# Nine split pages for eight, one split in advance, three raw pairs for four, and two query blocks moved behind the query/key blocks

## The chip, the cores and the metric

One core of a Trainium2 chip. The time is the device time of one execution in microseconds (us), smaller is better. TensorE (PE in the profile) multiplies, VectorE (DVE), ScalarE (ACT) and GpSimd (POOL) do the rest, SyncE (SP) issues most of the transfers. All data is float32; the large products run as float32r, in which a value is split into a rounded high part and a low remainder.

## The reference

One layer of a hybrid encoder block on x of 1024 tokens by 1024 channels. Cut to what matters:

```python
h = rms_norm(x, norm_w)
z = einsum('bsd,dc->bsc', h, w_in)          # q, k, v of 3 groups, gates, and the recurrence's inputs
for g, (window, dilation) in enumerate(((128, 1), (512, 4), (2048, 16))):
    q = rms_norm(z_q[g], q_norm_w[g]); k = rms_norm(z_k[g], k_norm_w[g])
    outs, maxes, dens = dilated_window_attention(q, k, v, bias, window, dilation)
o_a = merge(outs, maxes, dens);  y_a = (o_a * silu(g_a)) @ w_proj_a
o_b = rms_norm(scan(q_b, i_b, zf_fwd) + flip(scan(flip(q_b), flip(i_b), flip(zf_bwd)))) * silu(g_b)
y_b = o_b @ w_proj_b
out = x + (sigmoid(zgate_a) * y_a + sigmoid(zgate_b) * y_b) @ w_out
```

There are 24 attention heads of 64 channels (8 in each group) and 8 recurrence heads of 128.

## The kernel before, in words

**Products.** Every large product is made of three float32r matmuls: high by high, high by low, low by high. A weight page of 128 x 512 is loaded raw and split into `whi` and `wlo`. `Builder.split` does it: ScalarE copies the raw page rounded into `whi`; then VectorE or GpSimd subtracts (`b.low` is "dve" or "pool"), or, with `b.low = "dma"`, ScalarE writes minus the high part into `wlo` and GpSimd issues a DMA that adds the page from memory to it. The pages go through two rings of `RING` = 8 buffers, `hir` and `lor`, strictly in order: page k may be split when `k < freed + RING`, where `free_to` counts the pages that TensorE has done with. A ring of `RAWS` = 4 raw pages feeds them; each split asks for the next raw page.

**Order of the work.** The program is laid out by a planner (`Plan`, `Builder`), which books a modelled duration for each instruction and from that decides the order in which each engine gets its instructions. Work waits as a task (an engine, tiles that must be done, a priority, a condition on room) and goes out in `tick`; small products wait in `small` and go out in `burst`. Where a ring has no room, `until` lets modelled time pass until it has. On the chip each engine runs its instructions in the order so laid down and waits on semaphores for its data.

**The stages.** (1) The first value group: `u_products(0, d)` and `u_products(1, d)`, d from 0 to 7, multiply pages 0 to 7 with the unnormalised input of two halves of the tokens; the row scale comes later. After each step d of the second loop page d is freed and, for d under 7, `split_next_page` splits the next one, with `b.low = "dma"`. After the loop `b.auto()` hands the splitting to the planner. (2) The second and third value group (pages 8 to 15 and 16 to 23), in units of eight steps; beside the second, `sums_h` and its followers make the sums of the input's quadrants on VectorE, with `b.low = "dve"`. (3) The blocks, below. (4) The inputs of the recurrence, with the attention of the three groups put in between; the merge of the groups; the recurrence by heads; the two output projections.

**The blocks.** 27 blocks of 1024 tokens by 512 columns (or the like) are computed in seven products instead of eight, in the manner of Strassen. A block's steps are T1, T2, 21, T3, then step 11 of the next block, then 22 and T4; each is 12 matmuls with one split page. `start_quads` loads the raw quarters of a block into pairs from the ring `qraw` (`QRAW` = 4 buffers of 128 x 1024; one pair holds quarters 11 and 12, another 21 and 22) and makes the differences in place on VectorE, each followed by its split; the low parts of T2 and T4 are made on VectorE and the other five on GpSimd. Both pairs of a block are released with its last split, T4. `run_quads` runs the products. Step 11 is evacuated by ScalarE into a buffer p, T1 into c, T2 into u; VectorE adds 21, T3 and 22 to them, and T4 is evacuated by itself. T3 adds into the bank that T2 has been copied from. For query/key blocks p, c and u come from the ring `spare` (`SPARE` = 7 buffers, handed out in turn), for the others from `stage`, and their T4 from `spare`.

There are five kinds of blocks: `qk` (12 of them: queries and keys of a group), `sg` (sigmoid gates), `qb` (the recurrence's queries), `gb` and `ga` (gates that pass through Silu in `put_raw`). The list `blocks` gives their order. By number, from 0:

```
before: qk sg qk qk sg qk qb qk sg qk qb qk sg qk qb qk sg qk qk sg qk gb gb gb gb ga ga
```

**The norm of queries and keys.** Each `qk` block is followed, for each half of the tokens, by a chain: `squares` (ScalarE), `sq_sum`, `sq_high`, `sq_low`, `head_sums` (two matmuls into `nss`), `guess` (ScalarE: Ln, Exp, Square), `newton`, `norm_root` and two times `scaled` on VectorE, then stores to `qkD`. The chain uses a ring `ny` of four buffers: two in `squares`, three in `guess`. `scaled` releases the block's buffers in `spare`; the T4 part is copied into a raw page (`raw<-qA` in the profile). Ln and Exp are called with the table of `natural_log_exp_and_others` loaded at the start of the stage (`blocks_start`); Silu brings in another table.

Of the kernel before, what the change touches and what calls it, by code (L numbers as in the profile page):

```python
# [21 lines left out]
NEG = -1e30  # L22
TABW = 384
WARM = 10
RING = 8
RAWS = 4
LEAD = 4
TAIL, LATE = 4, 4
EARLY = 8
QB = 6  # L30
QRAW, SPARE = 4, 7
RES = (1, 4, 16)
LOWS = ("T2", "T4")
SQ, EA = 2, 6
# [198 lines left out]
class Builder:  # L233
# [94 lines left out]
    def setup_weights(self, items, pool, ring, raws):  # L328
        self.RING = ring
        self.wpages, self.windex, self.quads, self.steps = [], [], [], []  # L330
        n = 0
        for k, it in enumerate(items):
            if not isinstance(it, tuple):
                self.wpages.append(it)
                self.windex.append(n)
                n += 1
                continue
            m = len(self.quads)
            self.quads.append(it)
            more = k + 1 < len(items) and isinstance(items[k + 1], tuple)  # L340
            if k == 0 or not isinstance(items[k - 1], tuple):
                self.steps.append((n, m, "11"))
                n += 1
            for op in ("T1", "T2", "21", "T3", "+", "22", "T4"):
                if op != "+":
                    self.steps.append((n, m, op))
                    n += 1
                elif more:
                    self.steps.append((n, m + 1, "11"))
                    n += 1  # L350
        self.ops = n
        self.w = {}
        self.rawr = self.ring(pool, "raw", raws, [128, 512])
        self.hir = self.ring(pool, "whi", ring, [128, 512], F32R)
        self.lor = self.ring(pool, "wlo", ring, [128, 512], F32R)
        self.raws = []
        self.raw_next = 0
        self.split_next = 0
        self.freed = 0
        self.offered = None  # L360
# [12 lines left out]
    def offer(self, t, k):  # L373
        self.task("act", [t], self.split_next_page, 2, lambda: self.split_next == k and k < self.freed + self.RING)

# [37 lines left out]
    def start_quads(self, ring):  # L413
# [44 lines left out]
        def ready(k):  # L458
            eng, n, m, src, dst = work[k]
            if at[0] != k or (n is not None and (self.split_next != n or n >= self.freed + self.RING)):  # L460
                return False
# [190 lines left out]
def hybrid_block(ctx, tc, a, out):  # L652
    b = Builder(ctx, tc, a)
# [20 lines left out]
    def bank(name):  # L674
        t = b.bank.get(name=name)
        b.bank.done(t)
        return t
# [18 lines left out]
    qk = [("qk", g, hv, e) for g in range(3) for hv in range(2) for e in range(2)]  # L696
    sg = [("sg", 0, j) for j in range(0, 8, 2)] + [("sg", 1, j) for j in range(0, TAIL, 2)]
    blocks = []
    for k in range(6):
        blocks += qk[2 * k:2 * k + 1] + sg[k:k + 1] + qk[2 * k + 1:2 * k + 2] + ([("qb", 2 * k - 2)] if 0 < k <= QB // 2 else [])  # L700
    blocks += [("gb", k) for k in range(4)] + [("ga", 0), ("ga", 2)]

    def block_pages(kind, *at):
# [25 lines left out]
    items += [wpa[i] for i in range(8)]  # L729
    b.setup_weights(items, wpool, RING, RAWS)  # L730

# [83 lines left out]
    def inv_rms(k, ps):  # L815
        for j in range(4):
            t_.matmul(ps[:, j:j + 1], acc[k][:, 128 * j:128 * j + 128], ones[:, 0:1], start=True, stop=True)
        return rsqrt(b, tiny, ps[:, 0:4], 4, 1.0 / D, "x")

    def spread(r):  # L820

        dg = pre.tile([128, 512], F32, tag="sq", name=b.name("dg"), bufs=SQ).rearrange("p (a t) -> p a t", a=4)
        v_.tensor_tensor(dg, ident[:, None, :].to_broadcast([128, 4, 128]),
                                r[:, :, None].to_broadcast([128, 4, 128]), op=OP.mult)
        return dg

    def spread_out(dg):
        ps = bank("rB")
        t_.matmul(ps, ones, dg, start=True, stop=True)
        return ps  # L830
# [164 lines left out]
    def keep_u(j):  # L995
        a_.activation(uv[j], ups[0][j], AF.Copy)
# [18 lines left out]
    def root(k):  # L1015
        rs[k] = inv_rms(k, bank("ss"))
        rs["d", k] = spread(rs[k])

    def root_out(k):
        rs["B", k] = spread_out(rs["d", k])  # L1020
# [16 lines left out]
    for j in range(4):  # L1037
        keep_u(j)
    b.low = "dma"
    at = {0: {11: lambda: root(1)}, 3: {5: lambda: root_out(1), 11: lambda: root(0)}, 7: {5: lambda: root_out(0)}}  # L1040
    for d in range(8):
        u_products(1, d, at.get(d, {}))
# [1172 lines left out]
    def seven_weights(base, pages, order, along=None, by_dma=()):  # L2215
# [13 lines left out]
        def split(op, i):  # L2229
# [3 lines left out]
            def f():  # L2233
# [4 lines left out]
            work.append((op, "act", lambda: (op, i) in raw and b.when_all([raw[op, i]])  # L2238
                         and b.split_next == k and k < b.freed + b.RING, f))

# [321 lines left out]
def _build(arrays):  # L2562
    import concourse.bacc as _bacc
    nc = _bacc.Bacc("TRN2", target_bir_lowering=False, num_devices=1)
    args = {n: nc.dram_tensor(f"in_{n}_dram", v.shape, mybir.dt.from_np(v.dtype), kind="ExternalInput").ap()
            for n, v in arrays.items()}
    out = nc.dram_tensor("out_0_dram", (S, D), F32, kind="ExternalOutput").ap()
    with tile.TileContext(nc) as tc:
        hybrid_block(tc, args, out)
    return nc  # L2570
# [9 lines left out]
```

## Time and profile before

| | |
|---|---|
| median of 3 runs | 1433.92 us (1433.57 to 1437.22) |
| the profiled execution | 1435.38 us; its span, from the first to the last instruction, 1433.6 us |
| mean granted TensorE clock | 0.995 |
| TensorE busy | 1408.3 us, 98% of the span |
| VectorE, ScalarE, GpSimd busy | 918.0, 848.3, 349.5 us |
| bytes moved | 230.31 MB, mean 161 GB/s |

Lines of the profile begin with an engine; `out<-in` are the program's tile names without their numbers, then shapes and a count. A timeline line gives the start in us from the span's start, then the duration, the instruction, and in brackets the idle time before it and what ended it. A line of the list of waits gives the total, the number and the longest. A line of the table by windows gives the window, its length, busy time of PE, weight loads, DVE, ACT and POOL, the granted clock, the DMA share and GB/s. All instructions have the line of one helper, so groups are told by tiles. The blocks run from about 148 to 676 us.

### The profile page before, as it was taken

To read this page: it belongs to the slowest core of one execution; us is meant where nothing else is said; L and a number is where in the kernel's file an instruction comes from. 1 tells how busy PE (TensorE), PEld (TensorE's weight loads), DVE (VectorE), ACT (ScalarE), POOL (GpSimd) and SP (SyncE) were. 2 spreads that over 40 slices of the span, in tenths; PEclk is the share of its full clock that TensorE was granted. 3 is DMA by queue.
4 is the path that set the end of the run, shared out by engine and by line. 5 is a ranking of instruction groups with operands and counts; after the bars stand their busy time and mean duration, and the time that the engine had idled before them with its cause. 6 is when DMAs were issued, how large, how long until landed. Compare 5 with 4: busy or idle time off the path is not lost. (4 is left out here: it accounts for less than half of the span.)

```text
span 1433.6 us, 24071 instructions
## 1 busy us (share of the span) xinstructions
PE 1408.3 (98%) x8506; PEld 1170.7 (82%) x8506; DVE 918.0 (64%) x1890; ACT 848.3 (59%) x1837; POOL 349.5 (24%) x378
## 2 busy tenths in 40 slices
PE   9999999999999999999999999899999999999998
PEld 8778888888888888788778888688888888788887
DVE  6574556666666666542356647978878686358973
ACT  7642656655555565843586642667777684558461
POOL 0100434454433333243141110122123121001011
PEclk9999999999999999999999999999999999999999
DMA  6737566677744434533887239745445443768565
GB/s 225 176 105 212 163 204 160 150 182 174 169 131 118 103 89 98 158 112 117 286 282 254 94 85 273 209 109 126 103 118 126 123 131 87 236 231 220 176 170 143
DMA packets 200804, 230.31 MB, mean 161 GB/s; under 512 B 60531, under 2 KB 125323, under 8 KB 200172
## 3 DMA queue, kind: packets, MB, share of 16 engines
q1 hardware_dynamic: 182876, 193.19, 44.4%
q0 software_dynamic: 16944, 35.40, 13.2%
q8 instruction: 67, 1.10, 0.3%
q14 instruction: 53, 0.43, 0.1%
q10 hardware_dynamic: 864, 0.19, 0.1%
HBM read 168.77 MB, written 81.43 MB: 175 GB/s over the span
## 5 line engine op out<-in xcount | busy, mean ns | idle before, releaser
L60 POOL TENSOR_TENSOR wlo<-qraw,whi 128x512 fp32r<-128x512 f32 x135 | 181.2, 1344 | 390.5 <-ACT whi L60 383.8
L60 ACT ACTIVATE whi<-qraw 128x512 fp32r<-128x512 f32 x189 | 117.7, 626 | 101.6 <-POOL wlo L60 36.8
L60 PE MATMUL gp<-hh,whi 128*128 128x512 f32 x264 | 109.0, 413 | 0.0
L60 DVE TENSOR_TENSOR qraw<-qraw,qraw 128x512 f32<-128x512 f32 x81 | 70.0, 865 | 57.6 <-POOL wlo L60 57.6
L60 PE MATMUL gp<-hh,wlo 128*128 128x512 f32 x264 | 103.6, 392 | 0.0
L60 PE MATMUL gp<-hl,whi 128*128 128x512 f32 x264 | 103.0, 390 | 0.0
L60 ACT ACTIVATE whi<-raw 128x512 fp32r<-128x512 f32 x92 | 57.5, 626 | 75.8 <-DMA raw<-in_w_in_dram 38.3
L60 ACT ACTIVATE as<-as,neg 128x192 f32<-128x192 f32 (+1 forms) x192 | 77.8, 409 | 23.9 <-DVE neg L60 23.9
L60 PE MATMUL qA<-hh,whi 128*128 128x512 f32 x216 | 84.0, 389 | 0.0
L60 PE MATMUL qA<-hl,whi 128*128 128x512 f32 x216 | 84.0, 389 | 0.0
L60 PE MATMUL qA<-hh,wlo 128*128 128x512 f32 x216 | 84.0, 389 | 0.0
L60 PE MATMUL gp<-wlo,hh 128*128 128x512 f32 x192 | 76.0, 396 | 4.0 <-DMA wlo<-in_w_in_dram 3.0
L60 PE MATMUL gp<-whi,hh 128*128 128x512 f32 x192 | 79.6, 415 | 0.0
L60 PE MATMUL gp<-whi,hl 128*128 128x512 f32 x192 | 75.8, 395 | 0.0
L60 POOL COPY mm<-Bc 128x8 f32<-128x8 f32 x64 | 32.5, 543 | 171.6 <-DVE Bc L60 171.6
L60 POOL DMA_DIRECT2D wlo<-in_w_in_dram x36 | 31.1, 864 | 142.1 <-ACT wlo L60 92.3
L60 DVE CUSTOM_DVE_ANT_0 as<-sc,abias 128x192 f32<-128x192 f32 (+1 forms) x192 | 48.4, 308 | 21.3 <-PE sc L60 12.4
L60 PEld LDWEIGHTS gp<-hh,wlo 128*128 128x128 f32 x264 | 49.5, 188 | 10.9
L60 PEld LDWEIGHTS gp<-hh,whi 128*128 128x128 f32 x264 | 49.7, 188 | 8.9
L60 PEld LDWEIGHTS gp<-hl,whi 128*128 128x128 f32 x264 | 49.8, 189 | 8.3
L60 DVE TENSOR_TENSOR wlo<-qraw,whi 128x512 fp32r<-128x512 f32 x54 | 38.4, 711 | 28.2 <-ACT whi L60 28.1
L60 DVE TENSOR_TENSOR ny<-ny,spare 128x512 f32<-128x512 f32 x36 | 55.7, 1549 | 0.0
(316 smaller groups left out, 4123.5 us busy)
## 6 DMA issues: line engine op xcount, KB each, us to landing
raw<-in_w_in_dram SPq DMA_DIRECT2D x84, 256.0 KB, 3.1
qraw<-in_w_in_dram SPq DMA_DIRECT2D x60, 256.0 KB, 4.3
qraw<-in_w_in_dram SPq DMA_DIRECT2D x24, 512.0 KB, 4.4
qkD<-ny SPq DMA_DIRECT2D x192, 64.0 KB, 2.1
wlo<-in_w_in_dram POOLq DMA_DIRECT2D x36, 256.0 KB, 4.4
sg<-sgD SPq DMA_DIRECT2D x32, 256.0 KB, 3.7
eraw<-wsD SPq DMA_DIRECT2D x32, 256.0 KB, 3.1
sgD<-stage SPq DMA_DIRECT2D x26, 256.0 KB, 2.2
```

Source lines behind the costliest of these rows:

```text
L60: got = f(*args, **kw)
```

## The change

`RING` goes from 8 to 9 in all stages: one more buffer in `whi` and one in `wlo`, 2 KB a partition each. `QRAW` goes from 4 to 3: one buffer of 4 KB a partition less in the stage of the blocks. Before the loop over `u_products(1, d)` one page is split in advance, with the low part by DMA. And of the three `qb` blocks that stood between `qk` blocks one stays there (block 9, where the first was block 6), and two go behind the last `qk` block:

```
after:  qk sg qk qk sg qk qk sg qk qb qk sg qk qk sg qk qk sg qk qb qb gb gb gb gb ga ga
```

```diff
-RING = 8
+RING = 9
-QRAW, SPARE = 4, 7
+QRAW, SPARE = 3, 7
...
     for k in range(6):
-        blocks += qk[2 * k:2 * k + 1] + sg[k:k + 1] + qk[2 * k + 1:2 * k + 2] + ([("qb", 2 * k - 2)] if 0 < k <= QB // 2 else [])
+        blocks += qk[2 * k:2 * k + 1] + sg[k:k + 1] + qk[2 * k + 1:2 * k + 2] + ([("qb", 0)] if k == 2 else [])
+    blocks += [("qb", h) for h in range(2, QB, 2)]
     blocks += [("gb", k) for k in range(4)] + [("ga", 0), ("ga", 2)]
...
     for j in range(4):
         keep_u(j)
     b.low = "dma"
+    b.split_next_page()
     at = {0: {11: lambda: root(1)}, ...}
     for d in range(8):
         u_products(1, d, at.get(d, {}))
```

## The prediction

> **What bounds the kernel now.** I read the page first, then the list of what TensorE waits for, then the timelines around its longest waits.
>
> ```profile
> span 1433.6 us, 24071 instructions
> ...
> PE 1408.3 (98%) x8506; PEld 1170.7 (82%) x8506; DVE 918.0 (64%) x1890; ACT 848.3 (59%) x1837; POOL 349.5 (24%) x378
> ```
>
> TensorE is busy 98% of the span. The change adds and removes no matrix product, so it can win only what TensorE loses: 1433.6 - 1408.3 = 25.3 us of idle time and what a lowered clock costs. All the rest is room to lose.
>
> ```profile
> PE kT L60 <- DVE sk L60: 3.9, 1, 3.9
> PE gp L60 <- DMA wlo<-in_w_in_dram: 3.0, 1, 3.0
> PE qA L60 <- ACT stage L60: 2.7, 1, 2.7
> PE sc L60 <- issue: 2.4, 1, 2.4
> PE al L60 <- DVE og L60: 1.8, 1, 1.8
> ```
>
> The columns are total, times, longest: each wait happens once. The second ends on a split page (`wlo`) and the third on ScalarE in the query/key stage: these the change can reach, and a shorter one on `wlo` below. The waits on `sk`, on the scores' first issue and on `og` end on other work of VectorE or on loads of the attention stage; one more split page does not feed them.
>
> **The ninth page and the page split in advance.** The 3.0 us wait, with its neighbours on TensorE, then the window that holds it, then ScalarE and GpSimd ahead of it:
>
> ```profile
> 58.34 0.39 PE L60 MATMUL gp<-whi,hh 128*128 128x512 f32 x1
> 61.68 0.80 PE L60 MATMUL gp<-wlo,hh 128*128 128x512 f32 x1 [2.95 <-DMA wlo<-in_w_in_dram]
> ...
> 65.06 0.40 PE L60 MATMUL gp<-whi,uhi 128*128 128x512 f32 x1
> ...
> 68.93 0.39 PE L60 MATMUL gp<-whi,ulo 128*128 128x512 f32 x1
> ```
>
> ```profile
> 60.00:80.00 20.00, 18.32 (x76) 14.29 (x77) 13.63 (x32) 10.62 (x27) 0.00 (x0) 0.91 0.55 136
> ```
>
> ```profile
> 50.16 0.63 ACT L60 ACTIVATE whi<-raw 128x512 fp32r<-128x512 f32 x1 [0.81 <-PE u L60]
> ...
> 54.96 0.62 ACT L60 ACTIVATE whi<-raw 128x512 fp32r<-128x512 f32 x1
> ```
>
> ```profile
> 51.75 0.86 POOL L60 DMA_DIRECT2D wlo<-in_w_in_dram  x1 [1.86 <-PE u L60]
> 56.54 0.86 POOL L60 DMA_DIRECT2D wlo<-in_w_in_dram  x1 [3.93 <-ACT wlo L60]
> ```
>
> From 65.06 to 68.93 there are 17 steps, 0.228 us each. The ninth matmul after the one at 58.34 would start at 60.39 at that pace and starts at 65.06: the stall costs 4.7 us. 61.68 - 58.34 - 0.23 = 3.1 us of it is waiting, the other 1.6 us is eight matmuls at about half pace (granted clock 0.91 in the window).
>
> The page awaited is page 15, the last of the second eight. With eight slots, pages 8 to 14 are split behind the eight steps of `u_products(1, d)`, and page 15 only after them, behind four evacuations: ScalarE at 54.96, the adding DMA issued at 56.54, landed at 61.68, so 5.1 us after its issue. With nine slots page 8 is split before the loop and every later page moves up one place: page 15 takes the place of page 14, ScalarE at 50.16 and DMA at 51.75, and is there at 51.75 + 5.14 = 56.9. It is needed at 58.57, so 1.7 us are left and the stall goes. What is late next is page 16, which is not needed before the next group of eight. The added split itself is 0.62 + 0.63 us of ScalarE and 0.86 us of GpSimd ahead of the loop; no page is split more often than before, the same work only stands earlier, and its raw page (loaded four ahead) needs no wait for a slot. If that cover failed, the next weight `hh` or `hl` would be up to 1.3 us late; I take nothing. Gain 4.7, bounds 3.1 (if this stall had met no clock drop) and 4.7.
>
> [...]
>
> The second page stall is in the next group, where VectorE makes the low parts:
>
> ```profile
> 106.29 0.39 PE L60 MATMUL gp<-whi,hh 128*128 128x512 f32 x1
> 107.71 0.50 PE L60 MATMUL gp<-wlo,hh 128*128 128x512 f32 x1 [1.04 <-DVE wlo L60]
> ```
>
> ```profile
> 103.96 0.69 DVE L60 TENSOR_TENSOR wlo<-raw,whi 128x512 fp32r<-128x512 f32 x1
> 104.56 2.49 DVE L60 TENSOR_TENSOR xs<-hh,hl 128x512 f32<-128x512 f32 x4
> 106.97 1.89 DVE L60 TENSOR_TENSOR wlo<-raw,whi 128x512 fp32r<-128x512 f32 x3
> ```
>
> It costs 107.71 - 106.29 - 0.23 = 1.2 us. One page earlier, the awaited page takes the place at 103.96, ahead of the four sums; its successor then takes the first place at 106.97, is ready about 107.6, and is needed three matmuls later, at 106.52 + 0.68 = 107.2. So 0.4 us of the wait stay: gain 0.7, bounds 0 and 1.2.
>
> **Three raw pairs for four.** The ninth page's room comes from one raw pair. A block's two pairs come free together after its last split. With three, the next block's second half loads only then. Of the blocks' loads the list of issues gives
>
> ```profile
> qraw<-in_w_in_dram SPq DMA_DIRECT2D x60, 256.0 KB, 4.3
> ```
>
> so it lands about 1.3 us of low part and 4.3 us of transfer later, 5.6 us, against two pages' time of 2 x 12 x 0.228 = 5.5 us: up to 2 us late with VectorE's difference behind it, once in a block. In the middle of the stage a split stands some 20 us ahead of its use (the eight slots, 2.7 us each), so this is hidden, and I take 0. Without that lead it would be at most 27 x 2 = 54 us; the ninth slot adds 2.7 us to it.
>
> **The query blocks.** The 2.7 us wait of `qA`, on ScalarE:
>
> ```profile
> 586.27 1.28 ACT L60 ACT_TABLE_LOAD   x1
> 587.57 0.69 ACT L60 ACTIVATE ny<-nss,eps 128x512 f32<-128x512 f32 x1
> 588.28 1.28 ACT L60 ACT_TABLE_LOAD   x1
> 589.57 1.29 ACT L60 ACTIVATE ny<-ny 128x512 f32<-128x512 f32 x2
> 590.77 0.58 ACT L60 ACTIVATE stage<-qA 128x512 f32<-128x512 f32 x1
> ```
>
> The logarithm and exponential of the last query/key block's norm run between the Silus of the first `gb` block, each with a table load of its own; the evacuation of T2 stands behind 4.5 us of this, and T3 waits for its bank. Two blocks without Silu put in between give the norm about 39 us more. The first Silu stays where it is, since block 21 stays the first `gb`. Gain 2.7, bounds 0 and 2.7.
>
> The moved blocks issue the same loads, splits and stores as before; SP's queue has the same transfers in another order, and the stored queries are read over 300 us later. But they no longer stand between query/key blocks, and there they gave the norm time. Rows of that chain, from the squares of a block to its last scaling:
>
> ```profile
> 499.30 1.14 ACT L60 ACTIVATE ny<-spare 128x512 f32<-128x512 f32 x2
> 532.85 1.14 ACT L60 ACTIVATE ny<-spare 128x512 f32<-128x512 f32 x2
> ```
>
> ```profile
> 296.45 1.78 DVE L60 TENSOR_TENSOR ny<-ny,spare 128x512 f32<-128x512 f32 x1
> ...
> 530.37 2.15 DVE L60 TENSOR_TENSOR ny<-ny,spare 128x512 f32<-128x512 f32 x1
> ...
> 569.36 2.17 DVE L60 TENSOR_TENSOR ny<-ny,spare 128x512 f32<-128x512 f32 x1
> ```
>
> ```profile
> L60 ACT ACTIVATE raw<-qA x12: 575/578/598, 170.2 to 560.6; 128x512 f32<-128x512 f32 x12
> ```
>
> ```profile
> 510.07 0.39 PE L60 MATMUL qA<-S2h,whi 128*128 128x512 f32 x1
> ```
>
> The T4 evacuations of blocks 0 and 20 lie 390.4 us apart: 19.52 us a block, T4(b) = 170.2 + 19.52 b. The chain of block 17 runs from 499.30, 2.8 us before T4(17) = 502.1, to 532.5, 30.4 us after it: 33.2 us. That of block 18 begins only then, at 532.85, and takes 38.7 us, to 571.5: with four `ny` buffers one block's chain does not overlap the next. Before, query/key blocks stood two blocks (39.0 us) apart, apart from two neighbouring pairs. After, they are blocks 0, 2, 3, 5, 6, 8, 10, 12, 13, 15, 16, 18: four pairs. And `spare` is handed out in turn, seven buffers: T1's copy in block 16 takes the buffer that block 13's chain releases last, T1's in 18 that of 15, T1's in 13 that of 10. TensorE feels it at T3 (at 510.07 in block 18, so T4(b-1) + 8.0), 1.2 us behind the two copies T1 and T2.
>
> With chains back on time at block 12: its chain ends at T4(12) + 30.4 = 434.8, block 13's runs from 435.2 to 468.4 (33.2 us) or 473.9 (38.7 us); block 16 wants the buffer at T4(15) + 6.8 = 469.8. So the cost is 0 to 4.1 us; I take 2. The last chain then ends before or just at the first Silu.
>
> **The sum,** against the profiled execution's 1435.38 us: 4.7 + 0.7 + 2.7 - 2 = 6.1 us, so 1429.3. That execution stands 1.5 us above the median of the three timed runs, 1433.92; against it the sum gives 1427.8 with the clock drop and 1429.4 without. I take 1428.
>
> **Rivals.** (1) The backlog of the norm chain never clears, and the kernel gets slower. The chain of block 5 ends at 298.2; block 6's could begin at T4(6) - 2.8 = 284.5, so it is 13.7 us late. A chain of 33.2 us makes up 5.5 us per two blocks, and by block 12 all is well. A chain of 38.7 us makes up nothing, and this is the duration the one late chain with the long scalings has (block 18, also 14 us late). Then block 10's ends at 365.4 - 2.8 + 14 + 38.7 = 415.3, against T4(12) + 6.8 = 411.2 wanted by block 13: 4 us. Block 12's ends at 454.4, just when block 15 wants it (450.3 and the 4 us lost). Block 13's ends at 493.5, against 469.8 + 4 wanted by block 16: 20 us. While TensorE stands, the splits do not disturb the chain, so a few us less: about 22 in all, 20 more than I take. 1428 + 20 = 1448, range 1440 to 1455. It decides from the point where chains take over about 36 us each. For it: block 18. Against it: block 3's chain, also late, took under 30 us.
> (2) Partly cleared: 5 to 10 us lost instead of 2, or the Silus still meet the last logarithm. 1431 to 1438, no change.
> (3) The change does not do what it says: page 15 is still late, because its DMA lands more than the 1.7 us later that are left, or the stalls only move to the next page. Then 1434 less what is left of the three gains, and with the 2 us of the chain: 1430 to 1434.
> [...] It would give 1426; chance 0.1, inside the likeliest case. [...]
>
> **Chances.** Likeliest case (1424 to 1431) 0.50, rival 1 0.22, rival 2 0.15, rival 3 0.13. No change means within 0.3%, about what a measurement of this kernel can tell: 1429.6 to 1438.2. From the likeliest case 0.42 are faster and 0.08 the same, from rival 2 0.13 the same and 0.02 slower, from rival 3 0.05 faster and 0.08 the same, rival 1 is slower: faster 0.47, same 0.29, slower 0.24. The range runs from 1423 (all gains, no backlog, less half clock) to 1444, into the lower part of rival 1.
>
> **What would show it.** Right: no wait on `wlo` near 58, page 15's DMA issued by 52, the clock 1.00 in that window; one table load at the first Silu and none between logarithm and exponential; no wait of `qA` over 2 us. Wrong: waits of `qA` on ScalarE at T3 of blocks 13, 15, 16 or 18, behind a copy into `spare` that follows a late last scaling; then rival 1. A split's lead under 10 us in the blocks would say that three pairs are too few.

## The result, and the profile after

| | before | after |
|---|---|---|
| median, same chip | 1434.62 us (8 runs, 1433.57 to 1437.92) | 1430.87 us (8 runs, 1427.17 to 1431.86) |
| ratio | 1 | 0.9964, 95% interval 0.9951 to 0.9977 |
| the profiled execution | 1435.38 us, span 1433.6 | 1428.14 us, span 1426.4 |

The ratio is that of the means (1435.2 and 1430.0 us): the kernel became faster by 0.36%, about 5 us (3.3 to 7.0). The medians lie 3.8 us apart. The forecast was 1428.0 with a range of 1423 to 1444. The profiled execution was one of the quicker ones: the median lies 2.7 us above it.

The page of the profile after, its head and the busy times:

```profile
span 1426.4 us, 24119 instructions
...
PE 1404.8 (98%) x8506; PEld 1166.4 (82%) x8506; DVE 934.6 (66%) x1889; ACT 840.9 (59%) x1831; POOL 358.4 (25%) x379
```

TensorE's idle time fell from 25.3 to 21.6 us. The list of what it waits for (total, times, longest):

```profile
PE kT L60 <- DVE sk L60: 3.6, 1, 3.6
PE qA L60 <- ACT stage L60: 2.1, 1, 2.1
...
PE nss L60 <- ACT nhi L60: 1.1, 1, 1.1
...
PE qA L60 <- ACT spare L60: 1.0, 1, 1.0
PE nss L60 <- DVE nlo L60: 0.9, 1, 0.9
PE sc L60 <- PE gp L60: 0.8, 1, 0.8
...
PE gp L60 <- DVE wlo L60: 0.4, 1, 0.4
```

The 3.0 us on page 15 (`DMA wlo<-in_w_in_dram`) is gone, and what was 1.0 us on the second page is 0.4. A wait of `qA` on ScalarE's `stage` of 2.1 us is still in the list, but it is another one: before, it stood at the first Silu (591 us), now it stands in the middle of the blocks (371 us), with three new companions there (`qA` on `spare`, and two of `nss`).

To see where the time went, I cut each span at the first and the last product of the blocks. From the timelines of TensorE, before and after:

```profile
147.86 0.39 PE L60 MATMUL qA<-hh,whi 128*128 128x512 f32 x1
...
675.80 0.39 PE L60 MATMUL qA<-hh,wlo 128*128 128x512 f32 x1
```

```profile
141.95 0.39 PE L60 MATMUL qA<-hh,whi 128*128 128x512 f32 x1
...
673.75 0.39 PE L60 MATMUL qA<-hh,wlo 128*128 128x512 f32 x1
```

| us | up to the blocks | the blocks | behind them | span |
|---|---|---|---|---|
| before | 147.9 | 527.9 | 757.8 | 1433.6 |
| after | 142.0 | 531.8 | 752.6 | 1426.4 |
| after, another execution | 142.1 | 532.8 | 755.0 | 1429.9 |
| new order alone, four pairs | 147.4 | 524.7 | 756.5 | 1428.7 |

(The last two, from the experiments below, were cut in the same way.) So the change won 5.9 us ahead of the blocks (some 0.5 us of it is spread between executions: the first `gp` product starts at 53.56 us before, at 52.99 after, and between 53.0 and 54.0 in the 14 profiles), **lost 3.9 us in the blocks**, and what lies behind them became 2.8 to 5.2 us shorter. The forecast had +5.4, +0.7 and 0.

**The new loss, read from the queues.** Around 370 us, first TensorE with its wait, then VectorE, ScalarE, SP's queue and GpSimd:

```profile
371.53 0.50 PE L60 MATMUL qA<-S2h,whi 128*128 128x512 f32 x1 [2.10 <-ACT stage L60]
```

```profile
358.10 1.20 DVE L60 TENSOR_TENSOR qraw<-qraw,qraw 128x512 f32<-128x512 f32 x1
...
368.63 0.69 DVE L60 TENSOR_TENSOR qraw<-qraw,qraw 128x512 f32<-128x512 f32 x1 [4.26 <-DMA qraw<-in_w_in_dram]
```

```profile
369.36 0.63 ACT L60 ACTIVATE whi<-qraw 128x512 fp32r<-128x512 f32 x1 [6.79 <-DVE qraw L60]
369.89 0.58 ACT L60 ACTIVATE stage<-qE 128x512 f32<-128x512 f32 x1
...
370.89 0.59 ACT L60 ACTIVATE stage<-qA 128x512 f32<-128x512 f32 x1
```

```profile
355.19 5.07 SPq L60 DMA_DIRECT2D qkD<-ny  x8
...
361.01 1.07 SPq L60 DMA_DIRECT2D qraw<-in_w_in_dram  x2
```

```profile
357.46 1.29 POOL L60 TENSOR_TENSOR wlo<-qraw,whi 128x512 fp32r<-128x512 f32 x1 [2.46 <-ACT whi L60]
```

```profile
386.19 0.39 PE L60 MATMUL qA<-S1h,whi 128*128 128x512 f32 x1
```

Read it backwards. T3 (`qA` at 371.53) may start once T2 has been copied out of its bank (`stage<-qA`, 370.89). That copy and T1's (369.89) stand in ScalarE's queue behind `whi<-qraw` at 369.36, for which ScalarE sat idle for 6.79 us. The split waits for VectorE's difference (368.63), idle for 4.26 us until a raw load had landed. That load was issued at 361.01, behind eight norm stores in SP's queue. The pair that it fills, the one of 21 and 22 of block 11, had been free since 359.30: GpSimd had made the low part of 22 (357.46 + 1.29 = 358.75), and VectorE had read 21 for the difference of T4 (358.10 + 1.20 = 359.30). So 1.7 us went by behind the stores, and 7.6 us from issue until VectorE could start. (The load does not wait for T4's own low part, so the block's two pairs do not come free at the same time: one block later this load is issued at 381.28 and T4's low part begins at 381.98.) In the window from 361.0 to 368.6 the DMA share is 0.98, at 231 GB/s, where over the blocks it is 0.54, at 141 GB/s; so the load shared DMA engines that were busy all the time. (That this made it slow is argued, not tested.) And the split that all this waited for is first used at 386.19, 17 us later. The late load harmed nobody who needed it; it harmed two evacuations that stood behind it.

### The profile page after: what moved, and what is told of

It reads as the page before. It is cut to its first block, busy times and chain, and to the rows that moved or that the text cites. A ratio compares the mean times of both kernels' runs of the same rounds, so it can differ in the third digit from the quotient of the medians.

```text
span 1426.4 us, 24119 instructions
## 1 busy us (share of the span) xinstructions
PE 1404.8 (98%) x8506; PEld 1166.4 (82%) x8506; DVE 934.6 (66%) x1889; ACT 840.9 (59%) x1831; POOL 358.4 (25%) x379
## 5 line engine op out<-in xcount | busy, mean ns | idle before, releaser
L60 POOL TENSOR_TENSOR wlo<-qraw,whi 128x512 fp32r<-128x512 f32 x135 | 189.4, 1410 | 378.6 <-ACT whi L60 370.1
L60 DVE TENSOR_TENSOR qraw<-qraw,qraw 128x512 f32<-128x512 f32 x81 | 83.2, 1028 | 47.2 <-DMA qraw<-in_w_in_dram 34.7
L60 DVE TENSOR_TENSOR ny<-ny,spare 128x512 f32<-128x512 f32 x36 | 48.2, 1348 | 0.3
```

The source lines that it names most:

```text
L60: got = f(*args, **kw)
```

## The experiments

Ratios are to the kernel before, run on the same chip in the same rounds (medians 1436.88, 1437.03, 1436.39 and 1436.12 us in the four groups).

**The changed kernel once more.** No edit; it gives the comparison for the others and a second profile.

> The changed kernel as it is, timed on the same chip as the next three. Ratio to the kernel before 0.9964 as in the first timing, about 1431 us. Both theories expect the same stalls of TensorE in the block stage as in its first profile (about 1.0 us at 349, 2.1 at 369, 1.1 and 0.9 near 478). If the times fall in two groups (1427 to 1428 and 1431 to 1432), a profile from the slower group should show more half clock or a longer stall.

Measured: 1431.25 us, ratio 0.9964 (0.9949 to 0.9978). Its blocks have stalls of the same kind (1.24 us at 252, 2.08 at 372, 0.89 at 482) and take 532.8 us. The loss in the blocks belongs to the kernel, not to one execution.

**All but the order.** Nine pages, the split in advance and three pairs, with the order of before:

```diff
-        blocks += ... + ([("qb", 0)] if k == 2 else [])
-    blocks += [("qb", h) for h in range(2, QB, 2)]
+        blocks += ... + ([("qb", 2 * k - 2)] if 0 < k <= QB // 2 else [])
```

> Nine pages, one split in advance and three raw pairs, but the blocks in the order of before. Theory A (the new stalls of the block stage come from three raw pairs: a load that is late blocks VectorE and ScalarE, and evacuations stand behind it): stalls of that kind stay, 2 to 5 us in all, and the 2.7 us at the first Silu comes back: about 1434 us. Theory B (the new stalls come from the crowded norm chains of the new order): only the 2.7 us at the first Silu is there, no other stall in the blocks: about 1429 us. Both: no stall near 58.

Measured: 1428.72 us, ratio 0.9943 (0.9930 to 0.9955). The time is theory B's, not A's.

**The order alone.** Eight pages, four pairs, no split in advance:

```diff
-RING = 9
+RING = 8
-QRAW, SPARE = 3, 7
+QRAW, SPARE = 4, 7
...
-    b.split_next_page()
```

> Only the order of the blocks is changed; eight pages, none in advance, four raw pairs. Theory A: no stall of TensorE over 0.3 us in the block stage, the stall near 58 as before: 1434.6 - 2.7 = about 1432 us. Theory B: the stalls of about 5 us in the blocks are there with four pairs too: about 1437 us.

Measured: 1430.15 us, ratio 0.9961 (0.9946 to 0.9976). Here A is right and B wrong. The order by itself won as much as the whole change. That is 5.6 us (3.4 to 7.8), more than the 3.2 us by which the blocks became shorter; in the profiled execution 0.4 us more lie ahead of the blocks and 1.2 us behind them, and whether that is more than the spread of executions is open.

**Three pairs alone.** The kernel before with `QRAW, SPARE = 3, 7`:

> Only the raw pairs are changed, three for four; eight pages, order of before. Theory A: stalls of qA on ScalarE behind a split that waits for its raw load, 2 to 5 us in all: about 1438 us. Theory B: no change, 1434.6 us, since the order of before leaves the chains their time and a split stands 19 us ahead.

Measured: 1434.75 us, ratio 0.9983 (0.9971 to 0.9995). Theory A's 1438 us did not come: in the order of before three pairs cost nothing.

Between them these settle who makes the loss. In one window that lies inside the blocks in every kernel (length, busy time of PE, weight loads, DVE, ACT, POOL), in this order: before, after, all but the order, the order alone, three pairs alone:

```profile
141.00:676.00 535.00, 532.26 (x2347) 440.19 (x2347) 313.99 (x387) 304.20 (x521) 212.77 (x173) 1.00 0.54 141
```

```profile
141.00:676.00 535.00, 529.84 (x2330) 436.66 (x2330) 327.42 (x382) 294.26 (x512) 218.15 (x172) 1.00 0.54 141
```

```profile
141.00:676.00 535.00, 531.93 (x2345) 439.44 (x2344) 320.55 (x382) 302.69 (x518) 217.02 (x172) 1.00 0.55 142
```

```profile
141.00:676.00 535.00, 535.00 (x2362) 442.98 (x2361) 310.71 (x386) 299.04 (x517) 214.95 (x174) 1.00 0.55 143
```

```profile
141.00:676.00 535.00, 532.14 (x2346) 439.52 (x2345) 308.73 (x387) 304.78 (x521) 220.90 (x173) 1.00 0.55 142
```

With the new order alone TensorE is busy for 535.00 of 535 us: the Silu stall is gone and nothing has come in its place. So theory B, that the crowded norm chains of the new order make the stalls, falls as long as there are four pairs. Three pairs alone leave 2.86 us idle, about what the Silu stall was before (2.74), and it is still the Silus, at 587 to 611 us, where it lies. Only both together give the 5.2 us of after. The effects don't add, which is what a queue would do. VectorE waits about as long for raw loads in all but the order (31.7 us, 15 times, by its list of waits) as in after (34.7 us, 12 times). The first has 0.7 us of stalls outside the Silus, the second 5.1: what counts is whether an evacuation happens to stand behind. With three pairs the order of before is if anything the quicker one (0.9943 and 0.9964).

**The split in advance left out.** Everything else as in the changed kernel:

```diff
-    b.split_next_page()
```

> The changed kernel without the one split page in advance; the ninth slots, three raw pairs and the new order stay. Theory (the prediction's step): the early stall is a matter of page 15's place in the order, and the ninth slot alone does not move it, since one page is split behind each step and page 15 still comes after the loop. Then the wait on wlo near 58 us is back with 2.6 to 3.1 us and about 1.6 us of half clock behind it, and the kernel is 3 to 5 us slower than with the split in advance (about 1434 to 1436 where the changed kernel gives 1431). Rival: the ninth slot alone does it, no wait over 1 us near 58, and the time is the changed kernel's within 1 us.

Measured: 1435.99 us, ratio 0.9996 (0.9980 to 1.0012), 0.0032 or 4.6 us above the changed kernel's. The wait is back:

```profile
PE gp L60 <- DMA wlo<-in_w_in_dram: 3.5, 1, 3.5
```

The theory holds: the ninth slot does nothing for page 15 without the advance.

**Raw loads first.** The changed kernel, with a higher priority for the loads of the raw pairs in the plan of SP's queue:

```diff
-                self.task("sp", [], lambda m=m, b=b: load(m, b), 2,
+                self.task("sp", [], lambda m=m, b=b: load(m, b), 0.5,
```

> The changed kernel, but the raw loads of the blocks get a higher priority in SP's queue than the norm's stores. Theory A (a raw load of the three pairs stands in SP's queue behind the stores of a norm chain that is not ready; the difference waits for it on VectorE, the split behind it on ScalarE, and the evacuations behind the split): VectorE's idle time ahead of the differences that a load ends falls from 38 us to under 10 us, no wait of qA on ScalarE over 0.5 us between 106 and 560 us, and 2 to 4 us are won against the changed kernel. Rival C (the load is late because the pair itself comes free late, one block's two pairs together, whatever stands ahead of it in SP's queue): that idle time stays above 25 us, stalls of 1 to 2 us of qA stay, and the time is the changed kernel's within 1 us.

Measured: 1430.38 us, ratio 0.9952 (0.9936 to 0.9969); not to be told from the changed kernel. VectorE still waits 34.1 us for raw loads (13 times), as rival C has it. But the edit did not do what it was for where it mattered:

```profile
354.97 5.07 SPq L60 DMA_DIRECT2D qkD<-ny  x8
...
360.79 1.07 SPq L60 DMA_DIRECT2D qraw<-in_w_in_dram  x2
```

The loads still come behind the eight stores (presumably since in the plan the pair comes free after them; this is not shown), and the stall at 371 us is there with 1.7 us. The run does not decide between the two theories. The rows above do in part: of the 9.3 us from the pair's release (359.30) to VectorE's start (368.63), 1.7 are spent behind the stores and 7.6 between issue and landing.

**Splits held back until their load is due.**

```diff
-            return all((m, x) in raw for x in src) and self.when_all([raw[m, x] for x in src])
+            return all((m, x) in raw and self.p.done(raw[m, x]) + 3.0 <= self.p.t["pe"] + self.AHEAD for x in src)
```

> The changed kernel, but a difference and its split are put into the queues only when the planner has the raw load landed 3 us before, so that ScalarE and VectorE are not held by a load. Theory A (the loss is in what stands behind the waiting split, not in the split itself, which is some 20 us ahead of its use): the idle time of VectorE ahead of the differences that a load ends falls to under half of 38 us, the waits of qA on ScalarE between 106 and 560 us go below 0.5 us, and 2 to 4 us are won. Rival D (the split is late for its own use, the pages' lead is too short): holding splits back makes it worse, waits of qA or its neighbours on whi or wlo appear, and the kernel is as slow as before or slower.

Measured: 1470.93 us, ratio 1.0233 (1.0210 to 1.0256). Rival D's outcome, and badly:

```profile
PE qA L60 <- ACT whi L60: 13.2, 11, 1.8
```

Holding a split back delays the release of its pair, so the next load, so the next split; the lead, measured from the end of a `whi` to the first product that uses it, falls from block to block and is 0.1 us from block 11 on, where the changed kernel keeps at least 16 us from block 1 on. Three pairs work only if each is used the moment it lands. That the splits must not wait in ScalarE's queue is not refuted by this, and not shown.

**Four pairs, with room taken from the norm.**

```diff
-QRAW, SPARE = 3, 7
+QRAW, SPARE = 4, 7
...
-        blk["lo"] = b.ring(p, "nlo", 2, [128, 512], F32R)
-        blk["hi"] = b.ring(p, "nhi", 2, [128, 512], F32R)
+        blk["lo"] = b.ring(p, "nlo", 1, [128, 512], F32R)
+        blk["hi"] = b.ring(p, "nhi", 1, [128, 512], F32R)
```

> The changed kernel with four raw pairs again; their room comes from the norm, whose high and low parts nhi and nlo get one buffer each for two. Theory A (three pairs and the new order together make the new stalls): no wait of qA on ScalarE over 0.5 us between 106 and 560 us, no idle time of VectorE that a raw load ends, and a time 2 to 4 us under the changed kernel's. Theory B (the crowded norm chains of the new order make them, with whatever pairs): the chains get longer by the missing buffers, and stalls of qA behind spare and of nss behind nhi and nlo stay or grow, 1 to 5 us in all, the time that of the changed kernel or above.

Measured: 1433.86 us, ratio 0.9971 (0.9958 to 0.9985). Each theory has its half. No `qA` waits for ScalarE any more; but the smaller rings bring stalls of the norm's own products, 5 us in all:

```profile
PE nss L60 <- ACT nhi L60: 2.1, 1, 2.1
PE nss L60 <- DVE ny L60: 2.1, 3, 1.0
```

**Page 15 without a ninth slot.** The new order, eight pages and four pairs; only the low part of page 15 is made another way, since before `b.auto()` stands one more line:

```diff
+    b.low = "pool"
     b.auto()
```

> Eight pages, four raw pairs and no split in advance, as before the change; the query blocks in the new order, and the low part of page 15 made by GpSimd's subtraction (1.3 to 1.5 us in the blocks) in place of the second ScalarE copy and a DMA of 5.1 us. Theory A (of the change only three raw pairs cost time, and the ninth page is needed for nothing but page 15): page 15 is there at about 54.9 + 0.6 + 1.5 = 57.0 us, needed at 58.6, so no wait on wlo near 58; no stall over 0.5 us between 108 and 590 us, one table load at the first Silu; the stall at 106 us stays with 1.0 us. The time is that of the new order alone (ratio 0.9961 to before) less 4.6 us: ratio about 0.993, some 3 to 5 us under the changed kernel's 0.9964. Rival (gains don't add: what is won early is lost at waits of the attention stage, on sc, al and kT, and at half clock after them): the stalls up to 690 us are gone all the same, but the ratio stays at 0.995 to 0.997.

Measured: 1428.31 us, ratio 0.9936 (0.9919 to 0.9953). ScalarE's one copy, then GpSimd's subtraction:

```profile
54.49 0.62 ACT L60 ACTIVATE whi<-raw 128x512 fp32r<-128x512 f32 x1
```

```profile
55.24 1.29 POOL L60 TENSOR_TENSOR wlo<-raw,whi 128x512 fp32r<-128x512 f32 x1 [3.11 <-ACT whi L60]
```

The page is there at 56.5 us where the transfer brought it at 61.7, the wait is gone, the blocks run without a stall (535.00 of 535 us busy), and the time is some 4 us under the changed kernel's (ratios 0.9936 and 0.9964, from two groups of runs, whose intervals just touch). It beats the kernel before clearly and the changed one by all appearance, with none of the buffers moved. A wait of 3.0 us on `sc`, now ended by the load of `av`, did come back: the rival is right on that wait, but not on the sum.

**The same one line in the order of before.**

> The kernel before with one edit: the low part of page 15 by GpSimd's subtraction. Theory (page 15's stall costs 4.7 us, by itself, and the last norm chain among the Silus 2.7 us, by itself): no wait on wlo near 58 us, the Silu stall stays with 2 to 3 us and two or three table loads, and 4 to 5 us are won against before, ratio 0.9965 to 0.997. Rival (the early stall can be taken away without gain, since a later wait that is set by loads grows by as much): the wait is gone and the ratio is 0.998 to 1.0, with longer waits on sc, al or kT.

Measured: 1432.19 us, ratio 0.9972 (0.9957 to 0.9986), 4.0 us by one line. The Silu stall stayed, with 2.6 us and three table loads around it (580.9 to 587.5 us).

**New order and three pairs with eight pages.** The order alone, and `QRAW, SPARE = 3, 7`:

> The new order and three raw pairs, with eight pages and no split in advance: the changed kernel without the ninth slot. Theory A (new order and three pairs alone make the block stalls): the blocks, from the first to the last of their products, take about 531.8 us as in the changed kernel (524.7 with the new order and four pairs), VectorE waits for raw loads for 30 us or more, and the ratio to before is about 1.000 (new order alone 0.9961, plus 7 us of 1436 lost in the blocks is 0.0049). Theory F (the ninth slot has its part: with nine the splits run further ahead, until the raw pairs and no longer the slots hold them, and so VectorE and ScalarE meet each load before it has landed; three pairs in the old order waited 24 us with eight slots and 105 us with nine): waits under 24 us, blocks within 3 us of 524.7, ratio 0.996 to 0.998.

Measured: 1435.39 us, ratio 0.9996 (0.9981 to 1.0012). The blocks take 529.1 us, 4.4 more than with four pairs, with VectorE waiting 35.5 us for loads, so theory A holds for the most part and F falls; the ninth slot and the split in advance add only the 2.7 us from 529.1 to 531.8, by one execution of each. (The 105 us on which F was built are the waits of all engines, 69.2 us of them GpSimd's idle time before its first page of the blocks. VectorE's own are 23.7 us with eight slots and 31.7 with nine.) Against the order alone three pairs cost 0.0035, 5 us.

**GpSimd also for the pages after.** The version with the one line, without the later `b.low = "dve"`:

> The new order with eight pages and four pairs, page 15's low part by GpSimd as in the version before, and GpSimd making the low parts also of the next pages (16 to 23), which VectorE made between its sums. Theory: the stall at 102 us (1.0 us, on a low part behind four sums on VectorE) is gone, since GpSimd does nothing from 60 to 125 us, and nothing else changes: 1.2 us less than with page 15 alone, ratio about 0.993, which is as much as a comparison here can hardly tell; the waits decide. Rival: subtractions on GpSimd and sums on VectorE at the same time slow each other (in the blocks GpSimd took 1.29 us when alone and up to 2.5 us), the sums end later, and the first block waits for them by more than 1 us.

Measured: 1431.20 us, ratio 0.9963 (0.9948 to 0.9978): a miss, in another way than the rival had it.

```profile
97.31 10.18 POOL L60 TENSOR_TENSOR wlo<-raw,whi 128x512 fp32r<-128x512 f32 x6
```

```profile
PE gp L60 <- POOL wlo L60: 2.8, 4, 0.7
```

Six subtractions in a row take 1.70 us each there, and TensorE, which asks for these pages faster than that, waits four times 0.7 us instead of once 1.0.

## Why the prediction was right, and where it was not

**Page 15: right.** Its place in the order, the copies and the transfer came out as worked out:

```profile
49.59 0.63 ACT L60 ACTIVATE whi<-raw 128x512 fp32r<-128x512 f32 x1 [0.81 <-PE u L60]
```

```profile
51.18 0.86 POOL L60 DMA_DIRECT2D wlo<-in_w_in_dram  x1 [1.86 <-ACT wlo L60]
```

ScalarE at 49.59 and GpSimd at 51.18 stand for the forecast 50.16 and 51.75, and the wait is gone. The size of 4.7 us is met by the two single tests, 4.6 us (left out of the changed kernel) and 4.0 us (cured otherwise in the kernel before), each to some 2 us. Nothing paid for the split in advance.

**The second page stall: right.** The forecast left 0.4 us of the wait; 0.35 us stayed.

**The query blocks and Silu: right, and a little more.** One table load remains at the first Silu, none between a logarithm and its exponential:

```profile
571.28 1.28 ACT L60 ACT_TABLE_LOAD   x1
```

The gain is what the order alone shows: blocks of 524.7 us for 527.9, 3.2 us, where the forecast had the 2.7 of the wait. So this stall cost its idle time and some 0.5 us more.

**Three raw pairs: the step that failed.** The forecast said "so this is hidden, and I take 0", since a split stands some 20 us ahead of its use. The mechanism behind it was right but for a detail: the second half of the next block loads only when T4's difference and the low part of 22 have set the pair free, a little ahead of T4's own split. Its size was not: "up to 2 us late" was 4.3 us of VectorE's idle time, because the load took 7.6 us from issue to landing, with the DMA engines busy for 98% of that time, and was issued 1.7 us late behind the norm's stores. The forecast had 4.3 us for it, from the row of the 256 KB loads; this is one of 512 KB, for which the page of before has 4.4. And the conclusion was wrong, since a lead covers only the reader of the split. The question that step never asked is what stands behind the waiting split in ScalarE's queue: evacuations that TensorE needs at once. Price: 4.4 us with eight pages (529.1 - 524.7), and 7.1 us together with the ninth slot in the changed kernel (531.8 - 524.7), where the forecast had nothing. Without the cure of page 15 nothing would be left of the change, as the kernel without the split in advance shows (0.9996).

The sign that the forecast named, a lead under 10 us, did not come; the lead was 16 us and more. It was the wrong sign to look at. The idle time of ScalarE ahead of a split would have been the right one.

**The norm chains: the size about right, the cause and place not.** I took 2 us for crowding in the new order, at T3 behind copies into `spare`. With four pairs it costs nothing. The claim under it, that "with four `ny` buffers one block's chain does not overlap the next", is wrong in the changed kernel. The squares of block 6 start at 279.93, 27 us before the last scaling of block 5; only its logarithm comes behind that:

```profile
279.93 1.13 ACT L60 ACTIVATE ny<-spare 128x512 f32<-128x512 f32 x2
...
307.21 0.69 ACT L60 ACTIVATE ny<-nss,eps 128x512 f32<-128x512 f32 x1
```

```profile
306.95 0.68 DVE L60 TENSOR_TENSOR ny<-ny,spare 128x512 f32<-128x512 f32 x1
```

So rival 1, the backlog that grows, falls, and with it the upper part of the range. Rival 2 had the right size of loss (5 to 10 us in the blocks) with the wrong cause, and rival 3 falls with page 15. What did come at 479 us reads as crowding set off by a late load:

```profile
465.83 0.69 DVE L60 TENSOR_TENSOR qraw<-qraw,qraw 128x512 f32<-128x512 f32 x1 [5.61 <-DMA qraw<-in_w_in_dram]
```

```profile
477.32 0.63 ACT L60 ACTIVATE ny<-spare 128x512 f32<-128x512 f32 x1 [1.22 <-DMA qkD<-ny]
```

```profile
479.05 0.50 PE L60 MATMUL nss<-nhi,headones 128*128 128x512 f32 x1 [1.12 <-ACT nhi L60]
480.42 0.50 PE L60 MATMUL nss<-nlo,headones 128*128 128x512 f32 x1 [0.87 <-DVE nlo L60]
```

VectorE loses 5.61 us to the load, the chain and its stores run late, the next chain's squares wait for the buffer in `ny` that these stores hold, and TensorE meets `nss` before its input: 2.0 us. This is read from the rows and not tested by itself. With the same order and three pairs but eight pages VectorE loses 2.9 us at that place, and TensorE nothing.

**The ninth slot behind the blocks: a term that was left out.** `RING` holds in every stage, and the forecast priced it ahead of the blocks alone. Behind them the seven profiles with eight slots took 756.1 to 759.8 us (mean 757.5), the six with nine 752.6 to 756.0 (mean 754.6). (The kernel with splits held back is left out.) One place shows where part of that lies, ScalarE at the start of the output projections, before and after:

```profile
1230.96 0.60 ACT L60 ACTIVATE stage<-gp 128x512 f32<-128x512 f32 x1 [0.81 <-PE gp L60]
1231.45 0.62 ACT L60 ACTIVATE whi<-raw 128x512 fp32r<-128x512 f32 x1
1232.11 0.63 ACT L60 ACTIVATE wlo<-whi 128x512 fp32r<-128x512 f32 x1
1232.64 2.70 ACT L60 ACTIVATE xh<-acc 128x512 fp32r<-128x512 f32 x5
```

```profile
1223.36 0.60 ACT L60 ACTIVATE stage<-gp 128x512 f32<-128x512 f32 x1 [0.80 <-PE gp L60]
1223.85 2.45 ACT L60 ACTIVATE xh<-acc 128x512 fp32r<-128x512 f32 x4
```

With eight slots a page's split stands between the evacuation `stage` and the copies into `xh`, and TensorE waits for `xh`: 1.1 to 1.6 us in all seven, at most 0.5 us in the six with nine, where the copies follow the evacuation at once. (That the split comes so late because it had to wait for its slot is argued from the plan, not shown.) By the means of these waits (1.46 and 0.30 us) that is 1.2 of the 2.9 us between the means; where the rest lies is not shown. (In the profile before the granted clock reads 1.00 behind this wait, from 1230 to 1240 us.) But two of the kernels differ in the slot alone, new order and three pairs with eight pages and the changed kernel without the split in advance. There the ninth slot wins 1.1 us behind the blocks (756.3 and 755.2), loses 2.1 us in them (529.1 and 531.2), by one execution of each, and the ratios are the same, 0.9996. So the slot by itself won nothing that these runs can tell; it pays by making room for the split in advance.

**The sum: right by luck, by misses that offset each other.** Ahead of the blocks 5.9 us for 5.4; in the blocks -3.9 for +0.7; behind them +2.9 on the mean for 0: 4.9 us, against 6.1 in the forecast and 5.2 (3.3 to 7.0) measured. The profiled execution had 2 us more behind the blocks than the mean. Among that is the wait of 2.4 us on the scores' first issue, now 0.8 us; it is absent in some variants and 1.2 or 3.0 us in others. Why it moves I did not settle. The 1426 us to which the prediction gave a chance of 0.1, with less half clock, was near the shortest execution of the changed kernel (1427.17). The profile before has a granted clock of 0.50 in three stretches inside its span (61.40 to 64.81, 696.30 to 699.71 and 931.80 to 938.62 us), that after in one (926.4 to 929.8). So at the `sk` wait, 3.9 us before and 3.6 after, there is 3.4 us less of it; in the second execution of the changed kernel that wait was 1.9 us. As the same stall met half clock in one execution and not in another (last section), this is not shown to be a gain of the change. No run shows what decides whether half clock follows a stall, which the 1.6 us between 1427.8 and 1429.4 and the less half clock in 1423 and 1426 count on; the profiles show the stretches named here and the two executions of the last section.

## What to carry to other kernels

A lead hides a late load from its own reader only (here it was 17 us, and T3, which does not read that split, lost 2.10): before calling a wait hidden, list what stands behind the waiting instruction in the same in-order queue, and who needs that. Take the cheapest cure for a late page first; one subtraction of 1.29 us on an idle engine did for page 15 what a ninth slot and a split in advance did, without a buffer that another stage had to give up. And when a forecast comes out right, compare it stage by stage, since the total can hide two misses of three to five microseconds; a ring that is made longer is longer in every stage.

## What the runs showed of the hardware

**The same stall met half clock in one execution and not in the other.** The stall at T3 of the changed kernel in its two executions, each in two windows of 3.4 us (the first row is the window with the stall, the second the one that follows):

```profile
369.99:373.40 3.41, 1.87 (x8) 1.56 (x9) 3.38 (x3) 1.49 (x3) 1.78 (x1) 1.00 0.26 56
373.40:376.82 3.42, 3.42 (x17) 2.82 (x16) 1.68 (x3) 3.25 (x6) 1.30 (x1) 1.00 0.47 101
```

```profile
369.80:373.20 3.40, 1.32 (x6) 0.82 (x5) 2.71 (x4) 2.12 (x4) 1.41 (x1) 1.00 0.23 53
373.20:376.60 3.40, 3.40 (x10) 2.66 (x9) 1.67 (x2) 2.30 (x5) 1.64 (x2) 0.50 0.42 86
```

A stall of 2.1 us each time. In the first execution TensorE was idle for 1.54 us of the first window, and the second ran at a granted clock of 1.00, with 17 matmuls; in the other it was idle for 2.08 us, and the second ran at 0.50, with 10 matmuls. By the granted clock that costs another 1.7 us, half of the 3.40 (an estimate). Why the one met half clock and the other did not is not shown. So the step from 3.1 to 4.7 us in my first term is what one execution had, the one profiled before, with a granted clock of 0.50 from 61.40 to 64.81 us; that others have it too is not shown. The eight runs of the changed kernel spread over 4.7 us (1427.17 to 1431.86); how much of that is half clock is not shown either.
